# A decoder block on one core: six gate_up blocks with five steps of seven products, six more sets of weight sums made ahead of time, and the rotation's halves exchanged on ScalarE

## The chip, the cores and the metric

The kernel runs on one NeuronCore of a Trainium2 chip, in one launch. The metric is the device time of that launch in microseconds. The engines are named as the profile names them: PE (TensorE, matmuls), PEld (its weight loads), DVE (VectorE), ACT (ScalarE), POOL (GpSimd) and SP (SyncE, which here issues most of the DMA transfers; ACT issues the rest).

## What is computed

One decoder layer for 256 tokens of width 2048, all in float32: a norm, one combined projection to 17,408 columns, three groups of dilated attention with rotary positions, a gated linear recurrence, two branch products under gates, an output product, and a feed-forward network of width 5632. Cut to what the change touches:

```python
def rotary(t, seq_len):
    ...
    rot = jnp.concatenate([-tf[..., half:], tf[..., :half]], axis=-1)
    return (tf * cos + rot * sin).astype(t.dtype)
...
        proj = a @ w_in[layer]
        ...
        y = jax.nn.sigmoid(gate_a) * (attn @ w_attn_branch[layer]) + jax.nn.sigmoid(gate_r) * (r_out @ w_hgrn_branch[layer])
        h = h + rmsnorm(y @ w_mix_out[layer], norm_mix_post[layer])

        a = rmsnorm(h, norm_ffn_pre[layer])
        gt, up = jnp.split(a @ w_ffn_gate_up[layer], [D_FF], axis=-1)
        ...   # silu(gt) * up, times w_ffn_down, norm, added to h
```

## The kernel before

**Products in three parts.** PE multiplies in a reduced form of float32. To keep the precision, each operand is split into a high part (a copy to the reduced type, on ACT) and a low part (the difference, on DVE), and each product is three matmuls: high by high, high by low, low by high. Splitting the weights as they stream in is the steady work of ACT and DVE.

**Wide steps.** The output product and the feed-forward network are computed in wide blocks: two groups of 512 weight columns for all 256 tokens, in steps of 256 rows of the weights. A plain step is 2 token halves x 2 column groups x 2 row tiles, 8 products, 24 matmuls of 128x512. A step "by seven" treats the same as a 2x2 by 2x2 block product in Strassen's manner (Winograd's form): 7 products, 21 matmuls, at the price of sums of weight blocks and of activation blocks. Its weights come in two groups: four sums or blocks split into `w` and `wl`, and three raw blocks split into `dh` and `dl`. `multiply_wide` runs the products with the sums first, then those with the raw blocks, except in a block's last step by seven and in the down product, where the raw ones come first.

**Two ways to get the weight sums.** In the order tables, a step is (row pair, mode): mode 0 is plain; in mode 1 DVE makes the sums when the step is prepared; in mode 2 they were made long before. `weight_sums` does the latter, early in the program: it loads 1 MB of weights, does four DVE operations of 128x512, and stores the set to DRAM through ACT's queue. It is a generator; `ahead_of_time` moves it on by one `yield` for each of the 176 chunks (steps of the first projection and the two branch products). `fetch_sums` brings a set back four steps before it is used.

**The order of the work** is the order in the code; each engine works through its own list. In step i the main loop calls `prepare(i)`, which issues the split of step i + 2, the fetch of sums for step i + 4 and the raw load for step i + 5 (three raw slots), then `multiply(i)`, and then side work. After the second step of each gate_up block, `turn_act` transposes the activations of the block before into two banks of the pool from which the by-seven products get theirs; ACT empties them (L1349), and they are stored. `gather` and `evac_ffn` put the sums of a block together (L510 to L514), then silu and the multiplications (L1385). `dh` and `dl` share room for two steps, `sum` has room for one, `w` and `wl` for three.

**The rotation.** `evac_rope` finishes q and k tiles of 128x512. For the exchanged halves it multiplies 64 partitions of the source by the sine table into the other 64 of the result, twice, on DVE.

In the wide steps of `split_wide` the lines are: L418 (ACT) and L420 (DVE) plain; L426, L427, L429, L430 with fetched sums; L434, L440, L441 (sums on DVE), L439, L442, L445 (ACT), L447, L449 (DVE) with sums on the fly. In the changed kernel these lines stand 15 lower in the file (L420 is L435, L449 is L464), `turn_act`'s L1349 is L1365, L1385 is L1401.

Of the kernel before, what the change touches and what calls it, by code (L numbers as in the profile page):

```python
# [20 lines left out]
P = 128  # L21
S = 256
# [19 lines left out]
    [(2, 0), (3, 0), (0, 1), (4, 0), (1, 1), (5, 0), (6, 0), (7, 0)],  # L42
]
GATE_UP3 = [(3, 0), (4, 0), (0, 2), (5, 0), (1, 1), (6, 0), (2, 2), (7, 0)]
GATE_UP4 = [(4, 0), (5, 0), (0, 2), (6, 0), (1, 1), (2, 2), (3, 1), (7, 0)]
PLACE = (0, 2, 1, 3)
DOWN = [[(m, m in by7) for m in range(KF // 2)] for by7 in (range(4, 20, 3), range(3, 19, 3))]

N_F, N_RAW, N_SPLIT, AHEAD, WARM, BRIDGE = 15, 3, 3, 2, 8, 6

# [50 lines left out]
def tile_hybrid_block(ctx: ExitStack, tc: tile.TileContext, t, out):  # L101
# [13 lines left out]
    def nm(s):  # L115
        serial[0] += 1
        return f"{s}_{serial[0]}"
# [173 lines left out]

    pre, pre_in = {}, {}

    def weight_sums(jobs):

        for n in jobs:
            x = fp[0].tile([P, 2048], F32, tag="pre", bufs=1, name=nm("pre"))
            b, i = steps[n][:2]
            m = b.order[i][0]
            for g in range(2):  # L300
                nc.sync.dma_start(
                    x[:, g * 1024 : (g + 1) * 1024].rearrange("p (k c) -> p k c", k=2),
                    b.w[2 * m * P : (2 * m + 2) * P, b.cols[g] : b.cols[g] + 512]
                    .rearrange("(k p) c -> p k c", p=P),
                )
            for _ in range(4):
                yield
            r = [x[:, q * 512 : (q + 1) * 512] for q in range(4)]
            nc.vector.tensor_sub(r[2], r[2], r[0])
# [6 lines left out]
            nc.scalar.dma_start(pre[n], x)  # L316
            yield

    def fetch_sums(i):
# [7 lines left out]
    def ahead_of_time():  # L327

        if fp and back and not hold[0]:
            advance(back)  # L330

    def split(i):
        if i < len(items):
# [203 lines left out]
    def pair_sums(src, out, slot, pairs=H7):  # L537

        for m in pairs:
            f = ptile("f").rearrange("p (k t) -> p k t", k=2)  # L540
            x = src.slots[m]
            nc.vector.tensor_add(f, x[:, :, 0, :].bitcast(F32), x[:, :, 1, :].bitcast(F32))
            dst = slot().rearrange("p (z n t) -> p z n t", z=2, n=4)
            yield
            for part in seven_sums(f, dst):
                yield
                part()
            out[m] = sums_of(dst)
            yield
# [98 lines left out]
    back, hold = deque(), [False]  # L648
# [46 lines left out]
    def opening():  # L695
        ss, s2 = small("ss"), small("s2")
        yield from sumsq(ss, xt)
        nc.sync.dma_start(gainr, t["hgrn_norm_gain"].to_broadcast([P, HW]))
        nc.sync.dma_start(cs, t["rope"])
        add_parts(s2[:, :2], ss)  # L700
        rsqrt_mean(r1c, s2[:, :2], D)
        ready.add("r1c")
        nc.scalar.preload_act_table_set("silu_and_others")
        yield from row_broadcast(rowb, r1c)
        ready.add("rowb")
        yield
        for _ in range(24):
            yield
        for i, (j, c) in enumerate(((0, -QSCALE), (1, -QSCALE), (0, 1.0), (1, 1.0))):
            nc.vector.scalar_tensor_tensor(  # L710
                out=tabs[:, i, :], in0=cs[:, j, :], scalar=c, in1=rowb, op0=OP.mult, op1=OP.mult
            )
            yield
        nc.sync.dma_start(amask, t["amask"])
        nc.sync.dma_start(lmask, t["lmask"])
# [157 lines left out]
    def evac_rope(key, tab, then=None):  # L873

        cos = tabs[:, tab, :]
        sin = tabs[:, tab + 1, :]

        def ev(i, src):
            if i == 0:
                qkT[key] = fslot("qk").rearrange("p (h t) -> p h t", h=4)  # L880
            yield
            w = ptile("w").rearrange("p (h t) -> p h t", h=2)
            for o, n in ((0, 64), (64, 0)):
                nc.vector.tensor_mul(
                    w[o : o + 64], src[n : n + 64],
                    sin[n : n + 64, None, :].to_broadcast([64, 2, S]),
                )
            yield
            u = src
            nc.vector.tensor_mul(u, src, by_rows(cos, 2))  # L890
            nc.vector.tensor_add(
                qkT[key][:, 2 * i : 2 * i + 2, :].rearrange("p h (two j) -> p h two j", two=2),
                u.rearrange("p h (j two) -> p h two j", two=2),
                w.rearrange("p h (j two) -> p h two j", two=2),
            )
            if i == 1 and then:
                then()
        return ev
# [339 lines left out]
    def mix_to_ffn(i):  # L1238
# [60 lines left out]
        ffn(2, 1)  # L1299
        residual_of(5, (0, 1), False)  # L1300

    def more_h(c):
# [209 lines left out]
    def y_sums():  # L1512
        while not {0, 1} <= yT[0].there:
            yield
        yield from pair_sums(yT[0], y7, lambda: rslot("so"), (0, 1))

    def make_room(c):
        if c == 2:
            flush(evacs)
            flush(back)  # L1520
            end_phase1()

    early = [
# [31 lines left out]
        add("N", w_in, KD, COL_GA + 512 * j, xT, evac_gate(("a", j)))  # L1555
    for j in range(4):
        add("N", t["w_hgrn_branch"][0], 8, 512 * j, lambda k: recT[0](k), evac_rec_branch(j),
            pre=begin_branches if j == 0 else None)
# [13 lines left out]
    add_wide_block(w, (0, FF), PLAIN, lambda k: hT[0](k), None, evac_first, True, mid=more_h)  # L1572
    spare = wides[-1], 0
    for j in range(1, 11):
        add_wide_block(w, (512 * j, FF + 512 * j), GATE_UP4 if j > 1 else GATE_UP3, lambda k: hT[0](k),
                       lambda m: h7[m], evac_ffn, j % 2 == 0,
                       pre=begin_wides if j == 1 else None, turn=1)
    for j in range(2):
# [5 lines left out]
    back.append(  # L1584
        weight_sums([n for n, (b, i, *_) in enumerate(steps) if b.order[i][1] == 2])
    )

    load_x(0, 0, 256)
    load_wide(0, ((0, (0,)), (0, (1,))))
# [8 lines left out]
    split(1)  # L1598
    load_upto(AHEAD + N_RAW - 1)
    for i in range(len(items)):  # L1600
        kind, n, _ = items[i]
# [99 lines left out]
```

## Time and profile before

| | |
|---|---|
| median of 3 runs | 1697.41 us (1697.04 to 1697.93) |
| the profiled execution | 1698.13 us |
| its span | 1696.3 us |
| PE / PEld / DVE / ACT busy | 99% / 84% / 85% / 54% |
| granted TensorE clock, mean | 0.998 |
| DMA | 413.48 MB, 244 GB/s over the span |

Times in the profile are microseconds from the start of the span; the launch takes 1.8 us besides. The chunks end near 1000 us, then come the output product, eleven gate_up blocks (the first all plain) up to about 1455, two down blocks, and the end with its norm and stores from 1682. A row of a timeline gives start, duration, engine, line, operation, output and inputs, and in brackets the idle time ahead of it and what ended it.

### The profile page before, as it was taken

What the parts mean: (1) busy time and instruction counts of PE and PEld (TensorE: products, weight loads), DVE (VectorE), ACT (ScalarE), POOL (GpSimd) and SP (SyncE); (2) the same over time, 40 slices, a digit from 0 to 9 for tenths busy, and PEclk for the clock granted to TensorE, in tenths of its full rate; (3) what the DMA queues carried; (4) which work ended last, traced back from release to release, by engine and by line L of the source; (5) the groups of instructions that cost most, each with busy time, mean ns of one, the idle gap of its engine ahead of it and who ended that gap; (6) DMA issues with size and microseconds to landing.
All of it is one profiled execution on the core that took longest, in us unless ns stands there. A gap on an engine that the chain in (4) does not pass through costs nothing.

```text
span 1696.3 us, 21711 instructions
## 1 busy us (share of the span) xinstructions
PE 1685.2 (99%) x8260; PEld 1416.7 (84%) x8260; DVE 1436.2 (85%) x1662; ACT 914.7 (54%) x1034; POOL 3.9 (0%) x13
## 2 busy tenths in 40 slices
PE   9999999999999999999999999999999999999997
PEld 7888888888888888888888888888888888888886
DVE  6999888867998988885668888888888888898997
ACT  6655555544444434445445547555555555565663
POOL 0000000000000000000000000000000000000000
PEclk9999999999999999999999999999999999999999
DMA  8667666768677767787858646777777777777773
GB/s 285 205 224 243 230 233 228 234 222 309 225 254 252 256 223 243 253 310 275 295 172 275 210 162 227 269 250 252 254 255 253 249 248 272 257 266 256 248 244 130
DMA packets 228904, 413.48 MB, mean 244 GB/s; under 512 B 12816, under 2 KB 79552, under 8 KB 226240
## 3 DMA queue, kind: packets, MB, share of 16 engines
q1 hardware_dynamic: 218544, 373.93, 65.4%
q10 hardware_dynamic: 10192, 38.15, 6.0%
q8 instruction: 64, 1.05, 0.3%
q14 instruction: 40, 0.33, 0.1%
q0 software_dynamic: 64, 0.02, 0.0%
HBM read 376.92 MB, written 35.13 MB: 243 GB/s over the span
## 4 chain that ended last, share of the span: by engine, by line
PE 98%; DVE 1%; ACT 0%; issue 0%; DVEq 0%; ACTq 0%
PE acc L138 62%; PE aux L138 34%; PE aux L930 0%; DVE wl L420 0%; PE aux L610 0%; PE aux L1348 0%; DVE fz L1475 0%; PE acc L1348 0%; ACT w L418 0%; ACT junk L1429 0%; PE aux L597 0%; DVE e L1425 0%; PE aux L1110 0%; DVE yT L578 0%; PE aux L1220 0%
## 5 line engine op out<-in xcount | busy, mean ns | idle before, releaser
L138 PE MATMUL acc<-xT,w 128*128 128x256 f32 (+1 forms) x2048 | 366.8, 338 | 0.0
L420 DVE TENSOR_TENSOR wl<-raw,w 128x2048 fp32r<-128x2048 f32 (+1 forms) x141 | 306.6, 2182 | 68.8 <-ACT w L418 67.1
L138 PEld LDWEIGHTS acc<-xT,w 128*128 128x128 f32 x2048 | 311.9, 188 | 44.7 <-DVE w L365 0.3
L418 ACT ACTIVATE w<-raw 128x2048 fp32r<-128x2048 f32 (+1 forms) x141 | 256.3, 1827 | 109.3 <-PE acc L138 35.1
L364 ACT ACTIVATE w<-raw 128x1024 fp32r<-128x1024 f32 x176 | 185.7, 1058 | 220.5 <-PE acc L138 169.6
L365 DVE TENSOR_TENSOR w<-raw,w 128x1024 fp32r<-128x1024 f32 x176 | 214.8, 1221 | 95.9 <-ACT w L364 95.2
L138 PE MATMUL acc<-w,xT 128*128 128x512 f32 x578 | 169.1, 392 | 0.0
L439 ACT ACTIVATE w<-sum 128x1024 fp32r<-128x1024 f32 x56 | 59.5, 1063 | 177.8 <-DVE sum L434 170.6
L138 PE MATMUL acc<-w,hT 128*128 128x512 f32 x472 | 152.7, 391 | 0.4 <-DVE hT L1232 0.4
L447 DVE TENSOR_TENSOR wl<-sum,w 128x1024 fp32r<-128x1024 f32 x112 | 134.8, 1221 | 13.2 <-ACT w L439 13.2
L138 PEld LDWEIGHTS acc<-w,xT 128*128 128x128 f32 x578 | 108.1, 188 | 22.2
L138 PE MATMUL aux<-w,hT 128*128 128x512 f32 x374 | 120.0, 389 | 0.0
L449 DVE TENSOR_TENSOR dl<-raw,dh 128x1536 fp32r<-128x1536 f32 x56 | 98.3, 1756 | 14.3 <-ACT dh L445 12.2
L138 PE MATMUL aux<-w,xT 128*128 128x512 f32 x344 | 109.8, 389 | 0.0
L138 PEld LDWEIGHTS acc<-w,hT 128*128 128x128 f32 x472 | 88.5, 188 | 19.0 <-DVE hT L1232 0.8
L138 PE MATMUL acc<-wl,hT 128*128 128x512 f32 x236 | 91.9, 389 | 0.0
L445 ACT ACTIVATE dh<-raw 128x1536 fp32r<-128x1536 f32 x56 | 82.7, 1476 | 8.0 <-PE aux L138 4.4
L138 PE MATMUL acc<-w,a 128*128 128x512 f32 x268 | 83.7, 389 | 0.0
L138 PE MATMUL aux<-w,a 128*128 128x512 f32 x268 | 83.7, 389 | 0.0
L138 PEld LDWEIGHTS aux<-w,hT 128*128 128x128 f32 x374 | 70.2, 188 | 14.6
L138 PE MATMUL acc<-w,so 128*128 128x512 f32 x234 | 78.8, 391 | 0.0
L138 PEld LDWEIGHTS aux<-w,xT 128*128 128x128 f32 x344 | 64.6, 188 | 13.4
(298 smaller groups left out, 2964.3 us busy)
## 6 DMA issues: line engine op xcount, KB each, us to landing
raw<-in_w_in SPq DMA_DIRECT2D x270, 512.0 KB, 4.8
raw<-in_w_ffn_gate_up SPq DMA_DIRECT2D x156, 512.0 KB, 4.8
raw<-in_w_ffn_down SPq DMA_DIRECT2D x88, 512.0 KB, 5.4
pre<-in_w_ffn_gate_up SPq DMA_DIRECT2D x40, 512.0 KB, 6.5
presum<-pre ACTq DMA_DIRECT2D x20, 1024.0 KB, 4.7
s<-presum SPq DMA_DIRECT2D x40, 512.0 KB, 7.0
raw<-in_w_mix_out SPq DMA_DIRECT2D x32, 512.0 KB, 4.9
act<-acts SPq DMA_DIRECT2D x22, 512.0 KB, 6.5
```

The source lines that it names most:

```text
L138: nc.tensor.matmul(ps, lhsT, rhs, start=start, stop=stop, skip_group_check=True)
L364: nc.scalar.activation(wh, raw, AF.Copy)
L365: nc.vector.tensor_sub(wl, raw, wh.bitcast(F32))
L418: nc.scalar.activation(hi[:, c], raw[:, c], AF.Copy)
L420: nc.vector.tensor_sub(lo[:, c], raw[:, c], hi[:, c].bitcast(F32))
L439: nc.scalar.activation(hi[:, :1024], s[:, :1024], AF.Copy)
L445: nc.scalar.activation(dhi, d, AF.Copy)
L447: nc.vector.tensor_sub(lo[:, c], s[:, c], hi[:, c].bitcast(F32))
L449: nc.vector.tensor_sub(dlo, d, dhi.bitcast(F32))
```

## The change

1. A new table GATE_UP5 with five steps by seven in a row, used for gate_up blocks 3, 4, 6, 7, 9 and 10 (blocks 2, 5 and 8 keep GATE_UP4 with four). Three of its five use sums made ahead of time, where GATE_UP4 has two, so 26 sets are made in place of 20.
2. The second down block has seven steps by seven in place of six, and takes over the activation sums that the first block made for the same rows.
3. In the rotation ACT copies the two halves across, and DVE multiplies all 128 partitions once; the signs move into the tables.
4. `weight_sums` starts a set every six chunks in place of seven once the first q is there, on odd chunks. The last two sets are made by a second worker, `beside`, in half tiles, from the second recurrence branch block on.
5. One more pair of activation sums of the normed rows.

```diff
+GATE_UP5 = [(5, 0), (6, 0), (0, 2), (1, 1), (2, 2), (4, 2), (3, 1), (7, 0)]
 GATE_UP4 = [(4, 0), (5, 0), (0, 2), (6, 0), (1, 1), (2, 2), (3, 1), (7, 0)]
-DOWN = [[...] for by7 in (range(4, 20, 3), range(3, 19, 3))]
+DOWN = [[...] for by7 in (range(4, 20, 3), (2, 4, 7, 10, 13, 16, 18))]
...
-    def weight_sums(jobs):
+    def weight_sums(jobs, halves=False):
         for n in jobs:
-            x = fp[0].tile([P, 2048], F32, tag="pre", bufs=1, name=nm("pre"))
+            quick = not halves and ("q", 0, 0) in qkT
+            while quick and count[0] % 2 == 0:
+                yield
+            if halves:
+                xs = [fslot("pre") for _ in range(2)]
+            else:
+                x = fp[0].tile([P, 2048], F32, tag="pre", bufs=1, name=nm("pre"))
+                xs = [x[:, g * 1024 : (g + 1) * 1024] for g in range(2)]
...
-            for _ in range(4):
+            for _ in range(3 if halves or quick else 4):
                 yield
...
         if fp and back and not hold[0]:
             advance(back)
+        if fp and beside[0]:
+            advance(beside[0])
...
-        for i, (j, c) in enumerate(((0, -QSCALE), (1, -QSCALE), (0, 1.0), (1, 1.0))):
+        for i, (j, c) in enumerate(((0, -QSCALE), (1, QSCALE), (0, 1.0), (1, -1.0))):
...
             for o, n in ((0, 64), (64, 0)):
-                nc.vector.tensor_mul(
-                    w[o : o + 64], src[n : n + 64],
-                    sin[n : n + 64, None, :].to_broadcast([64, 2, S]),
-                )
+                nc.scalar.activation(w[o : o + 64], src[n : n + 64], AF.Copy)
             yield
             u = src
             nc.vector.tensor_mul(u, src, by_rows(cos, 2))
+            nc.vector.tensor_mul(w, w, by_rows(sin, 2))
...
-            lanes[1].append(pair_sums(hT[0], h7, lambda: rslot("so"), range(4)))
+            lanes[1].append(pair_sums(hT[0], h7, h7_slot, range(5)))
...
-        if by7:
+        if by7 and m not in a7:
...
+    def begin_beside(c):
+        if c == 0:
+            beside[0] = deque([weight_sums(jobs[-2:], True)])
...
-        add_wide_block(..., GATE_UP4 if j > 1 else GATE_UP3, ...)
+        order = GATE_UP3 if j == 1 else GATE_UP5 if j in (3, 4, 6, 7, 9, 10) else GATE_UP4
+        add_wide_block(..., order, ...)
```

What each engine is given, in order, at three places. The first is ACT's list in gate_up block 3, from the silu of the block before (L1382, in the changed kernel L1398) on; `act` is the tile into which the two transposed banks go. Before:

```order
L1382 ACTIVATE e_9257<-e_9257,r2c 128x512
L1382 ACTIVATE e_9258<-e_9258,r2c 128x512
L426 ACTIVATE w_9301<-s_9227 128x1024
L426 ACTIVATE w_9301<-s_9228 128x1024
L429 ACTIVATE dh_9307<-raw_9199 128x1536
L418 ACTIVATE w_9344<-raw_9231 128x2048
L1349 ACTIVATE act_9379<-acc_9380 128x512
L1349 ACTIVATE act_9379<-acc_9386 128x512
```

And after the change, the same stretch:

```order
L1398 ACTIVATE e_9349<-e_9349,r2c 128x512
L1398 ACTIVATE e_9350<-e_9350,r2c 128x512
L441 ACTIVATE w_9393<-s_9319 128x1024
L441 ACTIVATE w_9393<-s_9320 128x1024
L444 ACTIVATE dh_9399<-raw_9291 128x1536
L454 ACTIVATE w_9440<-sum_9442 128x1024
L457 ACTIVATE w_9440<-sum_9442 128x1024
L460 ACTIVATE dh_9448<-raw_9323 128x1536
L1365 ACTIVATE act_9485<-acc_9486 128x512
L1365 ACTIVATE act_9485<-acc_9492 128x512
```

One copy that needs only a raw tile stood ahead of the two emptying copies; now three stand there, and two of them need sums from DVE.

The second is DVE's list in the same block, from the sums of the first on-the-fly step to the low part of the last one. Before:

```order
L434 TENSOR_TENSOR sum_9396<-raw_9268 128x1024
L440 TENSOR_TENSOR sum_9396<-raw_9268,sum_9396 128x512
L441 TENSOR_TENSOR sum_9396<-raw_9268,sum_9396 128x512
L447 TENSOR_TENSOR wl_9395<-sum_9396,w_9394 128x1024 x2
L449 TENSOR_TENSOR dl_9403<-raw_9268,dh_9402 128x1536
L427 TENSOR_TENSOR wl_9437<-s_9348,w_9436 128x1024
L427 TENSOR_TENSOR wl_9437<-s_9349,w_9436 128x1024
L430 TENSOR_TENSOR dl_9443<-raw_9311,dh_9442 128x1536
L434 TENSOR_TENSOR sum_9475<-raw_9352 128x1024
```

After, from the first on-the-fly step's low parts on:

```order
L462 TENSOR_TENSOR wl_9441<-sum_9442,w_9440 128x1024 x2
L464 TENSOR_TENSOR dl_9449<-raw_9323,dh_9448 128x1536
L442 TENSOR_TENSOR wl_9501<-s_9403,w_9500 128x1024
L442 TENSOR_TENSOR wl_9501<-s_9404,w_9500 128x1024
L445 TENSOR_TENSOR dl_9507<-raw_9360,dh_9506 128x1536
L442 TENSOR_TENSOR wl_9539<-s_9454,w_9538 128x1024
L442 TENSOR_TENSOR wl_9539<-s_9455,w_9538 128x1024
L445 TENSOR_TENSOR dl_9545<-raw_9407,dh_9544 128x1536
L449 TENSOR_TENSOR sum_9574<-raw_9458 128x1024
```

Between the two on-the-fly steps there are now two with fetched sums, and the `dl` of the second stands directly ahead of the last step's sums.

The third is SP's list near the end of the chunks, where `pre` are the loads of `weight_sums`, `raw` those of the chunks, and `gate` fetches of stored gates. Before:

```order
L269 DMA raw_6863<-in_w_hgrn_branch 128x2x512 x2
L301 DMA pre_6911<-in_w_ffn_gate_up 128x2x512 x2
L858 DMA gate_6914<-waits_1557 128x2x512
L269 DMA raw_6919<-in_w_hgrn_branch 128x2x512 x2
L858 DMA gate_6958<-waits_1560 128x2x512
L269 DMA raw_6963<-in_w_hgrn_branch 128x2x512 x2
L269 DMA raw_7012<-in_w_attn_branch 128x2x512 x2
L269 DMA raw_7072<-in_w_attn_branch 128x2x512 x2
```

After:

```order
L270 DMA raw_6961<-in_w_hgrn_branch 128x2x512 x2
L309 DMA pre_6986<-in_w_ffn_gate_up 128x2x512
L309 DMA pre_6987<-in_w_ffn_gate_up 128x2x512
L873 DMA gate_7008<-waits_1560 128x2x512
L270 DMA raw_7013<-in_w_hgrn_branch 128x2x512 x2
L309 DMA pre_7059<-in_w_ffn_gate_up 128x2x512 x2
L270 DMA raw_7067<-in_w_attn_branch 128x2x512 x2
L270 DMA raw_7128<-in_w_attn_branch 128x2x512 x2
L309 DMA pre_7174<-in_w_ffn_gate_up 128x2x512
L309 DMA pre_7175<-in_w_ffn_gate_up 128x2x512
L270 DMA raw_7181<-in_w_attn_branch 128x2x512 x2
L309 DMA pre_7228<-in_w_ffn_gate_up 128x2x512 x2
```

Four loads of sums (two of them in halves, the second worker's) now stand between the last raw loads of the recurrence branch and those of the attention branch, where one stood.

More of the change, by code (lines that the diff above doesn't have):

```diff
@@ L44 @@
 GATE_UP3 = [(3, 0), (4, 0), (0, 2), (5, 0), (1, 1), (6, 0), (2, 2), (7, 0)]
+GATE_UP5 = [(5, 0), (6, 0), (0, 2), (1, 1), (2, 2), (4, 2), (3, 1), (7, 0)]
 GATE_UP4 = [(4, 0), (5, 0), (0, 2), (6, 0), (1, 1), (2, 2), (3, 1), (7, 0)]
 PLACE = (0, 2, 1, 3)
-DOWN = [[(m, m in by7) for m in range(KF // 2)] for by7 in (range(4, 20, 3), range(3, 19, 3))]
+DOWN = [[(m, m in by7) for m in range(KF // 2)] for by7 in (range(4, 20, 3), (2, 4, 7, 10, 13, 16, 18))]
 N_F, N_RAW, N_SPLIT, AHEAD, WARM, BRIDGE = 15, 3, 3, 2, 8, 6
@@ L301, in weight_sums @@
                 nc.sync.dma_start(
-                    x[:, g * 1024 : (g + 1) * 1024].rearrange("p (k c) -> p k c", k=2),
+                    xs[g].rearrange("p (k c) -> p k c", k=2),
                     b.w[2 * m * P : (2 * m + 2) * P, b.cols[g] : b.cols[g] + 512]
@@ L305, in weight_sums @@
                 )
-            for _ in range(4):
+            for _ in range(3 if halves or quick else 4):
                 yield
-            r = [x[:, q * 512 : (q + 1) * 512] for q in range(4)]
+            r = [xs[q // 2][:, q % 2 * 512 : (q % 2 + 1) * 512] for q in range(4)]
             nc.vector.tensor_sub(r[2], r[2], r[0])
@@ L315, in weight_sums @@
             pre[n] = dram.tile([P, 2048], F32, name=nm("presum"))
-            nc.scalar.dma_start(pre[n], x)
+            if halves:
+                for g in range(2):
+                    nc.scalar.dma_start(pre[n][:, g * 1024 : (g + 1) * 1024], xs[g])
+                yield
+            else:
+                nc.scalar.dma_start(pre[n], x)
             yield
@@ L647, in tile_hybrid_block @@
     evacs, turns, lanes, queue = deque(), deque(), [deque(), deque()], deque()
-    back, hold = deque(), [False]
+    back, hold, beside, count = deque(), [False], [None], [0]
     ready = set()
@@ L1300, in mix_to_ffn, with h7_slot @@
         residual_of(5, (0, 1), False)
+    def h7_slot():
+        return p3("so", F32R, 1024, 4) if len(h7) < 4 else rslot("so")
     def more_h(c):
@@ L1520, in make_room @@
             flush(back)
+            flush(beside[0])
             end_phase1()
@@ L1557, in tile_hybrid_block @@
         add("N", t["w_hgrn_branch"][0], 8, 512 * j, lambda k: recT[0](k), evac_rec_branch(j),
-            pre=begin_branches if j == 0 else None)
+            pre=begin_branches if j == 0 else None, post=begin_beside if j == 1 else None)
     for j in range(4):
@@ L1574, in tile_hybrid_block @@
     for j in range(1, 11):
-        add_wide_block(w, (512 * j, FF + 512 * j), GATE_UP4 if j > 1 else GATE_UP3, lambda k: hT[0](k),
+        order = GATE_UP3 if j == 1 else GATE_UP5 if j in (3, 4, 6, 7, 9, 10) else GATE_UP4
+        add_wide_block(w, (512 * j, FF + 512 * j), order, lambda k: hT[0](k),
                        lambda m: h7[m], evac_ffn, j % 2 == 0,
@@ L1583, in tile_hybrid_block @@
     wides[-3].post = lambda c: fetch_act(c // 2) if c in (1, 3) else None
-    back.append(
-        weight_sums([n for n, (b, i, *_) in enumerate(steps) if b.order[i][1] == 2])
-    )
+    jobs = [n for n, (b, i, *_) in enumerate(steps) if b.order[i][1] == 2]
+    back.append(weight_sums(jobs[:-2]))
     load_x(0, 0, 256)
@@ L1600, in tile_hybrid_block @@
     for i in range(len(items)):
-        kind, n, _ = items[i]
+        count[0], (kind, n, _) = i, items[i]
         b, c = kind[n][:2]
```

## The prediction

> **What bounds the kernel now.** I read the page's totals first, then PE's list of waits, then the chain.
>
> ```profile
> span 1696.3 us, 21711 instructions
> PE 1685.2 (99%) x8260; PEld 1416.7 (84%) x8260; DVE 1436.2 (85%) x1662; ACT 914.7 (54%) x1034; POOL 3.9 (0%) x13
> PE 98%; DVE 1%; ACT 0%; issue 0%; DVEq 0%; ACTq 0%
> PE aux L138 <- DVE warm L162: 1.2, 1, 1.2
> PE acc L138 <- DVE hT L1232: 0.4, 1, 0.4
> PE acc L138 <- DVE gate L1147: 0.2, 1, 0.2
> 1163.09 10.88 PE acc L138 x48
> ```
>
> PE works 1685.2 of 1696.3 us and all its named waits come to 1.8 us, so PE's own work is the time: a matmul less is a gain, and every new wait of PE is a loss at its full length. The last row is two plain steps in the chain: 48 matmuls of 128x512 in 10.88 us, 0.2267 us each. A plain step (24) costs 5.44 us, a step by seven (21) costs 4.76, so a replaced step gives 0.68. Seven are replaced, six in gate_up and one in the down product: 7 x 0.68 = 4.76 us. These are the only matmuls that the change takes away. What is left to find is which waits come in for them.
>
> **A gate_up block with five steps by seven.** I take FFN block 4 of the trace, from 1162.9 us, as the pattern, and move its rows as the new order asks.
>
> ```profile
> 1189.00:1231.00 42.00, 42.00 (x191) 34.88 (x190) 36.78 (x33) 24.14 (x21) 0.00 (x0) 1.00 0.73 253
> 1169.47 1.28 DVE L1385 TENSOR_TENSOR e<-e,e 128x512 f32<-128x512 f32 x2
> 1170.67 2.28 DVE L420 TENSOR_TENSOR wl<-raw,w 128x2048 fp32r<-128x2048 f32 x1
> 1184.98 1.22 DVE L434 TENSOR_TENSOR sum<-raw 128x1024 f32<-128x1024 f32 x1
> 1186.23 0.69 DVE L440 TENSOR_TENSOR sum<-raw,sum 128x512 f32<-128x512 f32 x1
> 1186.95 0.69 DVE L441 TENSOR_TENSOR sum<-raw,sum 128x512 f32<-128x512 f32 x1
> 1181.04 2.35 DVE L427 TENSOR_TENSOR wl<-s,w 128x1024 fp32r<-128x1024 f32 x2
> 1183.31 1.75 DVE L430 TENSOR_TENSOR dl<-raw,dh 128x1536 fp32r<-128x1536 f32 x1
> 1187.56 2.44 DVE L447 TENSOR_TENSOR wl<-sum,w 128x1024 fp32r<-128x1024 f32 x2
> 1191.15 1.76 DVE L449 TENSOR_TENSOR dl<-raw,dh 128x1536 fp32r<-128x1536 f32 x1 [1.16 <-ACT dh L445]
> ```
>
> The first row is one block period (us, then busy PE, PEld, DVE, ACT, POOL, the granted clock, DMA share, GB/s). DVE works 36.78 of 42.0 us. The new block trades a plain split (L420, 2.28) for a split with fetched sums (L427 and L430, 2.35 + 1.75 = 4.10): 38.6 of 41.3 us, 93%. On average it fits; the order decides whether each result is in time.
>
> *Place A, the third step.* The block's fourth step is now one that makes its sums on the fly; before it was plain. ACT does that split ahead of the two copies that empty the banks of the transposes, and PE wants the first of those banks for the seventh matmul of step 3.
>
> ```profile
> 1174.44 1.09 ACT L1349 ACTIVATE act<-aux 128x512 f32<-128x512 f32 x2 [3.91 <-PE aux L1348]
> 1175.83 0.62 PE L138 MATMUL aux<-w,so 128*128 128x512 f32 x2
> 1186.29 1.06 ACT L439 ACTIVATE w<-sum 128x1024 fp32r<-128x1024 f32 x1 [3.69 <-DVE sum L434]
> 1187.68 1.06 ACT L442 ACTIVATE w<-sum 128x1024 fp32r<-128x1024 f32 x1 [0.33 <-DVE sum L441]
> 1177.85 1.48 ACT L445 ACTIVATE dh<-raw 128x1536 fp32r<-128x1536 f32 x1
> ```
>
> Now the copies start at 1174.44, and ACT had been idle 3.91 us. In the new order DVE can begin the sums where the plain subtraction stood, 1170.67, behind the multiplications of L1385. The rows of the later step give the offsets: sums end 2.66 us after their start (1186.95 + 0.69 - 1184.98), at 1173.33; the second copy of sums starts 0.04 later, 1173.37, dh about 0.96 on, 1174.33; the first emptying copy follows some 1.4 later, 1175.7, and takes a half of 1.09 to 0.6, 1176.3. PE wants the bank at 1175.83 + 0.23 = 1176.06. A wait of 0.25 to 0.3 us. Bounds: 0, if DVE starts its sums 0.3 earlier than here, and 0.57, if the raw tile is late by as much again (place C). I take 0.30: 6 x 0.30 = 1.80 us.
>
> *Place B, the last step by seven.* The parts dh and dl have room for two steps. Before, the steps by seven stood three in a row at most; now there are five. Let S be the end of the fourth step of the block (the second by seven).
>
> ```profile
> 1189.63 1.49 ACT L445 ACTIVATE dh<-raw 128x1536 fp32r<-128x1536 f32 x1 [0.89 <-PE aux L138]
> 1189.66 0.39 PE L138 MATMUL aux<-w,so 128*128 128x512 f32 x1
> 1194.64 0.39 PE L138 MATMUL acc<-dl,hT 128*128 128x512 f32 x1
> ```
>
> The first row is such a wait for room: ACT starts dh as PE's step ends (next step's first matmul at 1189.66). dl followed it at 1191.15 and was done at 1192.91, and PE wanted it at 1194.64: 1.73 us to spare. In the new order the sixth step's dh waits for S; its dl follows at S + 1.5 on DVE. Only then, in DVE's order, come the seventh step's sums (start S + 3.2, end S + 5.85), its second copy on ACT (S + 5.9), dh (S + 6.8 to 8.3), and dl (S + 8.35 to 10.1). The seventh step begins with the products of the raw weights, so PE wants dl at its second matmul, S + 2 x 4.76 + 0.23 = S + 9.75. A wait of 0.35 to 0.4 us; bounds 0 and 0.6 by the same rows with the gaps seen between them left out or doubled. I take 0.38: 6 x 0.38 = 2.28 us.
>
> *Place C, the block behind.* The raw tile of the next block's second step may be loaded only when that late dl has been read.
>
> ```profile
> 1192.94 0.88 SPq L287 DMA_DIRECT2D raw<-in_w_ffn_gate_up  x2
> raw<-in_w_ffn_gate_up SPq DMA_DIRECT2D x2, 512.0 KB, 4.1
> raw<-in_w_ffn_gate_up SPq DMA_DIRECT2D x156, 512.0 KB, 4.8
> 1199.38 1.92 ACT L418 ACTIVATE w<-raw 128x2048 fp32r<-128x2048 f32 x1 [2.12 <-PE acc L138]
> ```
>
> The load was issued 0.03 us after dl's end, its second half about 0.4 later, and landed 4.1 (these two) to 4.8 us (all) after that: S + 14.6 to 15.3. ACT's split is otherwise let in by PE, 4.7 us behind dl's wanted time in these rows (1199.38 against 1194.64), about S + 14.9 with the wait at B. So 0 to 0.5 us late, which reaches PE only where place A is tight too: in blocks 4, 7 and 10, which follow a block of five. I take 0.2: 3 x 0.2 = 0.60. The other four blocks have plain steps in those places, and time to make up what is late. The six more sets to fetch are 6 MB on SP's queue over ten blocks at share 0.73 of the DMA engines; I cost them at nothing, covered by the two steps of lead with which sums are fetched. More activation sums (one more pair for the normed rows) fall in the all-plain opening block, where DVE's fixed work is 8 x 2.2 of 43.5 us: nothing.
>
> **The down product.** One step more by seven.
>
> ```profile
> 1571.00:1696.00 125.00, 116.03 (x512) 95.73 (x511) 111.51 (x141) 68.54 (x78) 0.00 (x0) 0.98 0.60 205
> ```
>
> This row is the second block with the tail, where DVE has 13.5 us free. The step adds 1.22 + 2 x 0.69 + 2.44 + 1.76 - 2.28 = 4.5 us to DVE, and the activation sums of five steps are no longer made again. Its gain stays: -0.68, already in the 4.76. Bounds of a wait here: 0 to 0.3; I take 0.
>
> **The work ahead of time.** Six more sets, in less time for each, and the rotation's halves on ACT.
>
> ```profile
> 525.00:575.00 50.00, 50.00 (x289) 43.54 (x288) 46.62 (x70) 23.07 (x33) 0.00 (x0) 1.00 0.71 243
> L365 DVE TENSOR_TENSOR w<-raw,w 128x1024 fp32r<-128x1024 f32 x96 | 117.0, 1220 | 32.0 <-ACT w L364 31.4
> L884 DVE TENSOR_TENSOR w<-sum,tabs 64x512 f32<-64x512 f32 x46 | 31.6, 687 | 1.0
> 613.67 1.02 SPq L301 DMA_DIRECT2D pre<-in_w_ffn_gate_up  x2
> 621.94 0.69 DVE L309 TENSOR_TENSOR pre<-pre 128x512 f32<-128x512 f32 x1 [0.40 <-issue]
> pre<-in_w_ffn_gate_up SPq DMA_DIRECT2D x40, 512.0 KB, 6.5
> ```
>
> The 525 to 575 row shows the tight part: DVE 93% busy, ACT 46%. A rotation costs DVE two multiplications of half the partitions (0.687 each) now and one of all of them after, 0.69 saved, 24 times: 16.6 us. Six sets at four times 0.69 cost 16.6 us. So DVE comes out even, and ACT, with half its time free, takes 48 small copies. A chunk lasts 315/96 = 3.28 us (the rows of L365 and L884 are from 437 to 752 us). A set's first subtraction now comes 8.3 us after its loads' issue and once waited 0.40 us; one chunk earlier it comes after 5.0, with 6.5 us and half the 1.02 of issue to wait for, so DVE stands some 2.0 us. About 2.5 sets fall into 50 us: 5 us, against 3.4 free and 2.5 saved by 3.65 rotations. It about fits, but the wait stands in front of chunk splits that PE wants soon. Bounds -0.5 (DVE freed of the rotations) to +6; near the lower one, +0.5.
>
> ```profile
> 792.00:812.00 20.00, 20.00 (x102) 16.93 (x101) 11.65 (x13) 10.48 (x14) 0.00 (x0) 1.00 0.93 304
> 812.00:832.00 20.00, 20.00 (x100) 16.89 (x99) 13.07 (x21) 10.46 (x14) 0.00 (x0) 1.00 1.01 363
> 832.00:852.00 20.00, 20.00 (x104) 17.04 (x104) 12.57 (x19) 8.53 (x12) 0.00 (x0) 1.00 0.62 203
> 852.00:872.00 20.00, 20.00 (x98) 16.84 (x97) 10.98 (x13) 8.11 (x9) 0.00 (x0) 1.00 0.53 178
> ```
>
> The last sets fall from 832 to 872 us, where SP's queue has the raw loads behind theirs. Three sets read and written are 6.3 MB on top of 7.6: 13.9 MB in 40 us, 348 GB/s. The row at 812 moved 363 with PE never idle, so I take +0.2; bounds 0 and, if only the 304 of the row at 792 can be had, 13.9 MB / 304 - 40 = +5.7.
>
> **The sum** against the profiled execution (1698.13 us, span 1696.3): -4.76 + 1.80 + 2.28 + 0.60 + 0.5 + 0.2 = +0.62, so 1698.75. The median of the runs, 1697.41, lies 0.72 below that execution; as a median I predict 1698.0.
>
> **Rivals.** (1) Only PE counts: the new waits at A and B are not there, as each rests on offsets of a few tenths. For it: PE is 99% busy. Against it: DVE at 93% in such a block, and a chain of single results. The gain is then whole, 1697.41 - 4.76 = 1692.65; with 0.7 lost in the early work, 1693.3. The Trainium skill ("Perfetto Trace Analysis", section "Identifying the Most-Contended Engine") says to improve first the engine with the highest occupancy, and by that rule this rival's time would come out; it also counts TensorE by its weight loads, here 84% beside DVE's 85%, by which DVE would be no less the bound. No row here decides between the two.
> (2) Slower, by the transfers of 832 to 872 us: the loads of sums stand ahead of raw loads on SP's queue, and it decides from where a raw load slips by more than its lead. A chunk there is 12 matmuls, 2.72 us, and three raw slots less 4.8 us of landing leave 3.4 us. The price is 5.7 less 3.4 to 5.7 whole, middle 4.0: 1698.0 + 4.0 = 1702.0. For it: share 0.93 at only 304 GB/s; against it: 363 right after. The Trainium skill (same page, section "Engine Utilization") puts the 16 DMA engines at some 435 GB/s for one active core; by that figure 348 would leave room and this rival would fall, but share 1.01 at 363 here speaks against taking it.
> (3) Slower, by the closer sets in the rotations' stage: beyond 2.4 us of wait for a set (5.9 free / 2.5) DVE falls behind. At 3.7 us (0.40 + 3.3) it loses 2.5 x 3.7 - 5.9 = 3.3 in 50 us, over the hundred tight microseconds 6.6; half of the sets so, about +3.5: 1701.5.
>
> **Chances.** Forecast 0.55, with its own range 1696.0 to 1700.5 (A and B together from 2.0 to 5.8). Rival 1 0.20, rival 2 0.13, rival 3 0.08, others 0.04, halved to both sides. What a measurement here tells from no change is about 0.2%, 3.4 us: faster 0.22, same 0.55, slower 0.23. The range for 8 in 10 takes in rival 1 after the early loss and most of rivals 2 and 3: 1693.0 to 1702.3.
>
> **What would show it.** Right: PE waits of 0.25 to 0.6 us once in each of blocks 3, 4, 6, 7, 9, 10 for ACT's emptying copy (now L1365), and of 0.3 to 0.5 for dl (L464); the period of such a block 42.0 us or a little less. Wrong: periods near 41.3 and no such waits (rival 1); PE waits or gaps from 832 to 875 us for a split whose raw load is late (rival 2), or from 525 to 640 us for L365's successor behind a waiting subtraction of a set (rival 3). A wait in the down product, or a changed clock, would be something that I have not priced.

## The result and the profile after

The changed kernel takes 1713.26 us (median of 4 runs, 1711.83 to 1714.02), the kernel before 1697.67 (4 runs): 1.009 of it, interval 1.0078 to 1.0103. The prediction was 1698.0 with a range to 1702.3, so the change costs 15.6 us where +0.6 was forecast. The profiled execution took 1712.61 us.

The page of the changed kernel, the totals and the chain:

```profile
span 1710.8 us, 21793 instructions
PE 1687.3 (99%) x8239; PEld 1410.2 (82%) x8239; DVE 1444.3 (84%) x1665; ACT 953.8 (56%) x1093; POOL 3.9 (0%) x13
PE 78%; DVE 8%; issue 5%; DMA 5%; ACT 3%; SPq 0%; DVEq 0%; ACTq 0%
```

PE runs 21 matmuls less, as foretold, and the span is 14.5 us longer. PE's share of the chain fell from 98% to 78%: DVE and DMA have come into it. PE's waits, first from 400 to 1000 us, then from 1000 on (in total, times, longest):

```profile
PE acc L139 <- DVE w L380: 6.1, 9, 1.4
PE aux L139 <- DVE q L1053: 1.1, 1, 1.1
...
PE acc L139 <- DVE e L1395: 1.2, 1, 1.2
PE aux L139 <- ACT act L1365: 1.0, 2, 0.5
PE acc L139 <- DVE dl L464: 0.8, 3, 0.3
PE aux L139 <- DVE dl L464: 0.8, 3, 0.3
PE acc L139 <- ACT act L1365: 0.5, 1, 0.5
```

The second group holds the waits for the emptying copy (L1365, place A) and for dl (L464, place B), six for dl and three for the copy above the list's threshold. The first group is the larger loss: nine waits for L380, DVE's low part of a chunk's weights, while the sets are made. The first matmul of the output product, which follows the chunks, puts a date on it: it starts at 903.10 us before and at 913.82 after (the chunks end there, near 900 us and not near 1000). The changed kernel is 10.7 us behind at that point, having been 0.8 ahead at 340 us, so the early work lost 11.5 us; the other 3.8 come behind it. Why L380 is late, in four rows of DVE, ACT and SP around 580 us, one of DVE at 842 us, the chain of waits from 831 us (start, length, what), SP's wait ahead of the set's load at 538 us (in total, times, longest), and the loads issued at 830 us (KB each, us to landing):

```profile
573.20 2.62 SPq L309 DMA_DIRECT2D pre<-in_w_ffn_gate_up  x2
585.39 0.69 DVE L317 TENSOR_TENSOR pre<-pre 128x512 f32<-128x512 f32 x1 [4.12 <-DMA pre<-in_w_ffn_gate_up]
586.72 1.22 DVE L380 TENSOR_TENSOR w<-raw,w 128x1024 fp32r<-128x1024 f32 x1
589.75 2.22 ACT L379 ACTIVATE w<-raw 128x1024 fp32r<-128x1024 f32 x2 [6.11 <-DVE pre L321]
...
842.20 0.69 DVE L317 TENSOR_TENSOR pre<-pre,pre 128x512 f32<-128x512 f32 x1 [8.30 <-DMA pre<-in_w_ffn_gate_up]
...
831.07 9.56 DMA presum<-pre
840.69 5.45 DMA pre<-in_w_ffn_gate_up
...
SPq L309 <- DMA presum<-pre: 2.5, 1, 2.5
...
pre<-in_w_ffn_gate_up SPq DMA_DIRECT2D x2, 512.0 KB, 11.1
```

DVE reaches a set's first subtraction (L317) before the set has landed and stands 4.12 and 8.30 us. Behind it in DVE's list are the low parts of chunks (L380), and ACT stands too, since its list has the set's store, which needs DVE's last operation (6.11 us ahead of L379). The chain shows one cause of a late load: it may not be issued until the set before has been stored, and that store took 9.56 us. The load of 538.26 us was held so for 2.5 us, and DVE stood 2.41 us for it. The last row shows another cause: these loads had been issued and took 11.1 us. The windows of two stretches, 525 to 600 us and that of the last sets, 832 to 892, each for the kernel before and then for the changed one (columns as in the prediction):

```profile
525.00:600.00 75.00, 75.00 (x444) 65.65 (x443) 71.35 (x105) 32.42 (x44) 0.00 (x0) 1.00 0.76 255
...
525.00:600.00 75.00, 71.34 (x414) 61.05 (x414) 65.64 (x97) 37.55 (x55) 0.00 (x0) 1.00 0.72 243
...
832.00:892.00 60.00, 60.00 (x296) 50.45 (x296) 39.53 (x53) 25.45 (x32) 0.00 (x0) 1.00 0.55 181
...
832.00:892.00 60.00, 56.62 (x270) 45.54 (x269) 41.36 (x57) 23.35 (x30) 0.00 (x0) 1.00 0.93 322
```

From 525 to 600 us PE loses 3.7 us of busy time at no higher a DMA share. From 832 on the share rises from 0.55 to 0.93, and PE loses 3.4 us in the 60.

### The profile page after: what moved, and what is told of

Read it like the earlier page. It is cut to its first block, busy times and chain, and to the rows that moved or that the text cites. A ratio compares the mean times of both kernels' runs of the same rounds, so it can differ in the third digit from the quotient of the medians.

```text
span 1710.8 us, 21793 instructions
## 1 busy us (share of the span) xinstructions
PE 1687.3 (99%) x8239; PEld 1410.2 (82%) x8239; DVE 1444.3 (84%) x1665; ACT 953.8 (56%) x1093; POOL 3.9 (0%) x13
## 4 chain that ended last, share of the span: by engine, by line
PE 78%; DVE 8%; issue 5%; DMA 5%; ACT 3%; SPq 0%; DVEq 0%; ACTq 0%
PE acc L139 49%; PE aux L139 28%; DMA presum<-pre 3%; DMA pre<-in_w_ffn_gate_up 2%; DVE w L380 1%; ACT w L433 1%; DVE sum L449 1%; DVE wl L435 1%; DVE e L1395 1%; ACT dh L444 1%; ACT dh L460 1%; DVE sum L455 0%; DVE sum L456 0%; DMA raw<-in_w_in 0%; DVE e L1401 0%
## 5 line engine op out<-in xcount | busy, mean ns | idle before, releaser
L139 PE MATMUL acc<-xT,w 128*128 128x256 f32 (+1 forms) x2048 | 368.2, 338 | 2.9 <-DVE w L380 2.9
L139 PEld LDWEIGHTS acc<-xT,w 128*128 128x128 f32 x2048 | 311.7, 188 | 49.2 <-DVE w L380 5.0
L435 DVE TENSOR_TENSOR wl<-raw,w 128x2048 fp32r<-128x2048 f32 (+1 forms) x134 | 290.8, 2178 | 64.1 <-ACT w L433 62.3
L433 ACT ACTIVATE w<-raw 128x2048 fp32r<-128x2048 f32 (+1 forms) x134 | 242.9, 1822 | 98.3 <-PE acc L139 29.3
L379 ACT ACTIVATE w<-raw 128x1024 fp32r<-128x1024 f32 x176 | 185.0, 1057 | 190.0 <-PE acc L139 102.9
L380 DVE TENSOR_TENSOR w<-raw,w 128x1024 fp32r<-128x1024 f32 x176 | 214.3, 1221 | 80.5 <-ACT w L379 80.2
L139 PE MATMUL acc<-w,xT 128*128 128x512 f32 x578 | 169.5, 392 | 0.1
L139 PE MATMUL acc<-w,hT 128*128 128x512 f32 x430 | 139.8, 391 | 0.4 <-DVE hT L1245 0.4
L139 PEld LDWEIGHTS acc<-w,xT 128*128 128x128 f32 x578 | 108.0, 188 | 22.7 <-DVE w L380 0.6
L139 PE MATMUL aux<-w,xT 128*128 128x512 f32 x344 | 109.8, 389 | 0.0
L464 DVE TENSOR_TENSOR dl<-raw,dh 128x1536 fp32r<-128x1536 f32 x57 | 100.2, 1757 | 9.2 <-ACT dh L460 7.1
L139 PE MATMUL aux<-w,hT 128*128 128x512 f32 x332 | 107.1, 389 | 0.0
L139 PEld LDWEIGHTS acc<-w,hT 128*128 128x128 f32 x430 | 80.7, 188 | 17.4 <-DVE hT L1245 0.8
L139 PE MATMUL acc<-w,so 128*128 128x512 f32 x258 | 87.7, 392 | 0.8 <-ACT act L1365 0.5
L139 PE MATMUL acc<-w,a 128*128 128x512 f32 x268 | 83.8, 389 | 1.2 <-DVE e L1395 1.2
L139 PE MATMUL acc<-wl,hT 128*128 128x512 f32 x215 | 83.7, 389 | 0.0
L139 PE MATMUL aux<-w,so 128*128 128x512 f32 x240 | 81.7, 392 | 1.1 <-ACT act L1365 1.0
L139 PE MATMUL aux<-w,a 128*128 128x512 f32 x254 | 79.4, 389 | 0.0
L139 PEld LDWEIGHTS aux<-w,xT 128*128 128x128 f32 x344 | 64.6, 188 | 13.4
```

The costliest lines, as they stand in the source:

```text
L139: nc.tensor.matmul(ps, lhsT, rhs, start=start, stop=stop, skip_group_check=True)
L379: nc.scalar.activation(wh, raw, AF.Copy)
L380: nc.vector.tensor_sub(wl, raw, wh.bitcast(F32))
L433: nc.scalar.activation(hi[:, c], raw[:, c], AF.Copy)
L435: nc.vector.tensor_sub(lo[:, c], raw[:, c], hi[:, c].bitcast(F32))
L464: nc.vector.tensor_sub(dlo, d, dhi.bitcast(F32))
```

## The experiments

Each is set against the kernel before, timed beside it, whose median was 1697.5 to 1697.8 in all of them. They are told in an order that follows the argument.

**The two halves of the loss.** The first kernel keeps the later blocks and puts the early work back (20 sets at the old pace; steps without a set of their own take another's):

```diff
+    reuse = {n: jobs[k] for k, n in enumerate(jobs[20:])}
+    jobs = jobs[:20]
...
-            quick = not halves and ("q", 0, 0) in qkT
+            quick = False
```

> The changed kernel with the early work as before: 20 sets of weight sums at the old pace, no second worker; the rotation stays on ScalarE and all later blocks stay changed (six steps fetch another step's set, so six sets are left out). Theory M (the closer sets and the second worker lose the early 11.5 us; the later blocks lose 3.8): the early loss is gone, 1697.7 + 3.8 = 1701.5, within 1700.5 to 1703. Rival R (the rotation's copies on ScalarE lose the 5 us between 540 and 600 us): 1706 or more.

Measured: 1701.77 us (ratio 1.0023, 1.0014 to 1.0032). The second keeps the early work and puts the later blocks back (`order = GATE_UP3 if j == 1 else GATE_UP4`, the old down table):

> The changed kernel with gate_up and down blocks as before (GATE_UP4, six steps by seven in the second down block), all 26 sets still made, six of them unused. Theory M: the early loss stays whole, 1697.7 + 10.7 = 1708.4, within 1707 to 1710, and no wait of PE in the gate_up blocks. If the loss came from the later blocks: near 1698.

Measured: 1709.15 us (1.0068, 1.0056 to 1.0081). +4.1 and +11.4 make 15.5 of the 15.6: the parts add up. The third is the kernel before with the rotation alone:

> The kernel before with the rotation's halves on ScalarE alone. Theory M: no loss, 1697.7 within 0.7 (DVE has 0.69 us less per rotation, PE waited for nothing there). Rival R: the copies stand ahead of splits on ScalarE's list, so 2 to 5 us more, 1700 to 1703.

Measured: 1697.94 us (1.0001, 0.9992 to 1.0009). The rotation costs nothing and gives nothing; the early loss is that of the sets.

**What in the sets.** Without the second worker (`beside[0] = deque()`, 24 sets):

> The changed kernel without the second worker: 24 sets at the new pace, two steps fetch another step's set (two sets are left out). Theory M: of the early 11.5 us the 5 between 540 and 600 us stay, the 5.4 between 840 and 875 us shrink to 1 or less, since the two workers no longer stand in one another's way on the queues: 1713.3 - 4.7 = 1708.6. Rival: the new pace alone fills the queues there, and no more than 1 us is won: 1712.3.

Measured: 1707.29 us (1.0057, 1.0043 to 1.0071). Its windows and PE's waits in the early work (its lines stand one lower in the file, L381 is L380):

```profile
832.00:892.00 60.00, 60.00 (x296) 50.51 (x296) 42.68 (x58) 25.31 (x32) 0.00 (x0) 1.00 0.77 263
...
PE acc L139 <- DVE w L381: 1.4, 3, 1.0
PE aux L139 <- DVE q L1054: 1.1, 1, 1.1
```

PE loses nothing any more from 832 to 892 us; what stays, 3.5 us by the trace, lies between 540 and 600 us. So the two last sets, with the worker that makes them, cost the late loss. (Up to 800 us this kernel does what the changed one does, whose profile lost 6.1 us there: the early loss differs by some 2.5 us from one execution to another.) Next, the sets' four DVE operations a chunk later and in one piece, at the same pace:

```diff
-            for _ in range(3 if halves or quick else 4):
+            for _ in range(4):
                 yield
...
-            yield
+            if not (halves or quick):
+                yield
```

> The changed kernel with each set's four DVE operations a chunk later and in one piece; the pace (six chunks for a set), the number of sets and all transfers stay. Theory L (DVE stands in front of chunk splits because a set's loads wait for the store of the set before and land after the first subtraction's place): the 5 us between 540 and 600 us shrink to 1.5 or less, and of the 5.4 at 840 to 875 us half go: 1713.3 - 6 = 1707.3. Rival P (the pace itself, DVE's or the transfers' load, is too high there): 1712.5 to 1714.

Measured: 1707.92 us (1.0060, 1.0048 to 1.0073). The same work at the same pace loses 5.3 us less when DVE comes to it later: the standing in front of a late load costs that much, and DVE's load is the same. Some 6 of the 11.5 us stay by its trace, so this run does not show that the standing is all of it. Then the stores issued by GpSimd (`nc.gpsimd.dma_start(pre[n], x)`):

> The changed kernel with the stores of the sets issued by GpSimd in place of ScalarE. Theory L with both engines standing (ScalarE's list waits at the store for DVE's late operations, with chunk splits behind it): 2 to 4 of the early 11.5 us go, 1710.5. If only DVE's standing counts (the low parts come from DVE anyway): no more than 1 us, 1712.5 to 1714.

Measured: 1710.27 us (1.0071, 1.0057 to 1.0085). ACT's standing behind the store is worth about 3 us of it (its runs spread from 1708.02 to 1712.94), between 540 and 600 us; the late loss stays. Then only one set stored:

> The changed kernel with one store: the first set alone is stored and every later step with fetched sums takes it (25 stores are left out; loads and DVE operations stay). Theory L (a set's loads wait for the store before, land late, and DVE stands): the loads start some 5 to 8 us sooner against DVE's place, and the early 11.5 us shrink to 2 or less: 1703.5. Rival P (DVE's own load is too high): the loss stays, 1712 or more. Between them, 1707 to 1710, if what is late is as much the loads' own landing, beside the fetches of values, as the wait for the store.

Measured: 1702.54 us (1.0028, 1.0017 to 1.0040): with 10.7 us less, the early loss is gone (0.55 us left by the trace). That takes two things away at once, the wait of a load for the store before it and the stores' own traffic. So a kernel with as many bytes stored, read from another tile, for which no load has to wait:

```diff
-                nc.scalar.dma_start(pre[n], x)
+                for g in range(2):
+                    nc.scalar.dma_start(pre[n][:, g * 1024 : (g + 1) * 1024], tabs.rearrange("p a t -> p (a t)"))
```

> The changed kernel with every set's store reading the rotation's tables in place of the set (two stores of 512 KB each, so the same 26 MB are moved; what later steps fetch is not the sums). The loads of the next set then wait for no store, and ScalarE's list for no DVE operation of a set. Theory L (the wait of loads for the store, and the two lists that stand): the early loss nearly goes as with one store, 1702.5 to 1704. Rival T (the stores' traffic makes the loads and the chunks' raw loads late): the loss stays in great part, 1708 to 1712.

Measured: 1709.49 us (1.0061, 1.0048 to 1.0075). Theory L alone is not enough: by the medians 3.8 us go with the waits, and some 7 stay with the traffic. Windows from 832 us and the loads issued at 836 us, of this kernel (KB each, us to landing), and the same windows with one store:

```profile
832.00:892.00 60.00, 57.46 (x278) 46.97 (x277) 43.15 (x61) 22.91 (x28) 0.00 (x0) 1.00 0.89 317
pre<-in_w_ffn_gate_up SPq DMA_DIRECT2D x2, 512.0 KB, 12.2
```

```profile
832.00:892.00 60.00, 60.00 (x297) 50.45 (x296) 49.88 (x69) 25.36 (x32) 0.00 (x0) 1.00 0.68 235
```

At a share of 0.89 a load takes 12.2 us from its issue; at 0.68 PE loses nothing. The single runs of this kernel spread from 1705.65 to 1710.47, those of the kernel before over 0.9 us, and its profile has 3.4 us at a granted clock of 0.50 (last section), an estimated 1.7 us of what stays. No run of the three kernels overlaps with another's, so the waits and the traffic both count; the split into 3.8 and 7 is good to 2 us or so, and which of them is the larger stays open.

**The gate_up blocks.** The order of the five steps alone is changed:

```diff
-GATE_UP5 = [(5, 0), (6, 0), (0, 2), (1, 1), (2, 2), (4, 2), (3, 1), (7, 0)]
+GATE_UP5 = [(5, 0), (6, 0), (0, 2), (2, 2), (1, 1), (3, 1), (4, 2), (7, 0)]
```

> The changed kernel with the five steps by seven in another order: (0,2), (2,2), (1,1), (3,1), (4,2). The fourth step's split then needs no sums from DVE ahead of the emptying copies (place A), and the last step needs none behind a late dl (place B). Theory M (A and B are matters of order): the 6.96 us that the traces show there go, and some of the 1.3 at the start of the down product, 1713.3 - 7 to 8 = 1705.5 to 1706.5. Rival D (DVE's load in such a block is the bound, whatever the order): 1711 to 1713.

Measured: 1707.96 us (1.0064, 1.0050 to 1.0077), 5.3 less and not 7 to 8. PE's waits after 1000 us, the end of its last gate_up block, and the windows around it:

```profile
PE acc L139 <- DVE e L1395: 2.2, 1, 2.2
PE acc L139 <- DVE dl L445: 0.7, 1, 0.7
PE acc L139 <- DVE hT L1245: 0.4, 1, 0.4
...
1461.87 0.47 PE L139 MATMUL acc<-w,a 128*128 128x512 f32 x1 [2.19 <-DVE e L1395]
1463.23 0.63 PE L139 MATMUL acc<-wl,a 128*128 128x512 f32 x1
1463.66 1.05 PE L139 MATMUL acc<-w,a 128*128 128x512 f32 x2
...
1462.00:1465.50 3.50, 3.50 (x10) 2.74 (x11) 1.51 (x3) 3.00 (x4) 0.00 (x0) 0.56 0.89 282
```

Places A and B are gone from all blocks but the last, where DVE also has the down product's activations to split. It comes 2.19 us late to the sums that free the banks, and after that idle time PE works at a granted clock of 0.56 for 3.5 us. With the five-step blocks moved so that the last gate_up block has four (and the early work as in the first experiment):

```diff
-GATE_UP5 if j in (3, 4, 6, 7, 9, 10)
+GATE_UP5 if j in (2, 3, 5, 6, 8, 9)
```

> The order of the last run, the blocks with five steps moved to 2, 3, 5, 6, 8 and 9 so that the last gate_up block has four, and the early work with 20 sets at the old pace (six steps fetch another step's set, six sets are left out). Theory M: all waits of the gate_up blocks go, and so does the one at the start of the down product: 6 x 0.68 = 4.08 and 0.49 for the second down block, 1697.7 - 4.6 = 1693.1, within 1692.4 to 1694. Rival D (DVE falls behind wherever two such blocks follow each other): a wait of about 1 us in blocks 3, 6 and 9, so 1696.

Measured: 1693.33 us (0.9975, 0.9965 to 0.9984), theory M to 0.2 us. With order and place right, six blocks with five steps give nearly their full gain: from block 1 to block 10 the trace has 371.7 us for 375.2 before, 3.6 of the 4.1, and one wait for dl of 0.2 us. How far this goes was tried with three on-the-fly steps of the five, which need no further set, `(0, 2), (2, 2), (1, 1), (3, 1), (4, 1)` in blocks 3, 5, 7 and 9:

> A version without any further set: the early work with 20 sets at the old pace; gate_up blocks 3, 5, 7 and 9 take five steps by seven of which three make their sums on the fly: (0,2), (2,2), (1,1), (3,1), (4,1); seven steps by seven in the second down block. DVE then has 36.8 + 6.8 - 2.3 = 41.3 us of work for 41.0 in such a block, and 36.8 of 41.7 in the block behind it. Theory M (order decides, the next block makes it up): 4 x 0.68 + 0.49 = 3.2 less than before, 1694.4. Rival D (a block over its period makes PE wait): a wait of 0.5 to 1 us in each, 1697 to 1698.5.

Measured: 1705.26 us (1.0044, 1.0032 to 1.0057). Rival D, and dearer than it said:

```profile
PE aux L140 <- DVE dl L465: 5.2, 4, 1.3
PE aux L140 <- ACT dh L461: 3.1, 4, 0.8
```

Two waits in each of the four blocks (the lines stand two or one lower here): 8.3 us, before PE's time to start again. Load and order are not told apart here. The three on-the-fly steps stand in a row, and DVE takes 6.85 us for each (two begin their sums at 1226.01 and 1232.86) where PE takes 4.76 for a step; in the first of them it stood 1.32 us for a dh that had no room yet. So 38.6 us of DVE's work in a block of 41.0 do fit in a good order; that 41.3 fit in none is not shown.

**Two versions meant to be faster.** The first has 22 sets at the old pace:

> A version meant to be faster, complete: 22 sets at the old pace and no second worker, the new order in gate_up blocks 4 and 7 alone, seven steps by seven in the second down block, the rotation on ScalarE. Theory M: no early loss (two more sets fall where the transfers have room, 850 to 890 us), 2 x 0.68 + 0.49 = 1.85: 1695.9. If two more sets already fill the queues there: 1697 to 1699.

Measured: 1705.63 us (1.0047, 1.0034 to 1.0059). A miss of its own making: one wait, `PE acc L139 <- ACT w L379: 6.8, 1, 6.8`, at 870 us. The last set was not done when the pools change, where the rest of a worker runs in one go, so its operations stood right behind its loads. The second makes 23 sets, at the new pace outside the stretch from about 500 to 600 us, the last done in time:

```diff
-            quick = not halves and ("q", 0, 0) in qkT
+            quick = ("q", 0, 0) in qkT and not 118 < count[0] < 145
...
-GATE_UP5 if j in (3, 4, 6, 7, 9, 10)
+GATE_UP5 if j in (3, 6, 8)
```

> A version meant to be faster, complete: 23 sets, no second worker, the new pace outside the stretch of about 500 to 600 us and the old one in it, the last set done before the change of pools; the new order in gate_up blocks 3, 6 and 8, seven steps by seven in the second down block, the rotation on ScalarE. 3 x 0.68 + 0.49 = 2.53 less than before: 1695.1. If the pace in the rest of the early work loses too (0.6 us near 750 us in the changed kernel): 1696.

Measured: 1695.10 us (11 runs, 0.9984, 0.9975 to 0.9993): faster than both kernels, by 2.7 us (0.16%; its slowest run, 1695.89, is below the fastest of the kernel before, 1697.15) and by 18 us. Its windows there and its only waits:

```profile
832.00:892.00 60.00, 60.00 (x296) 50.41 (x296) 43.52 (x59) 25.35 (x33) 0.00 (x0) 1.00 0.69 234
PE aux L625 <- DMA x<-in_x: 1.4, 1, 1.4
PE aux L139 <- DVE warm L163: 1.2, 1, 1.2
PE acc L139 <- DVE hT L1245: 0.4, 1, 0.4
PE acc L139 <- DVE gate L1160: 0.2, 1, 0.2
```

## Where the prediction was right and where it was wrong

**The work ahead of time (+0.7 forecast, +11.4 measured): the step that failed.** Two terms of the sum were mis-sized: +0.5 for the sets in the rotations' stretch and +0.2 for those from 832 to 872 us. Both took a mean over a stretch (DVE's free time, the transfers' rate) for what one late load does to the list behind it.
- For the stretch of the rotations I let a load land 6.5 us after its issue, and its issue stand where the list has it. The pair issued from 573.20 on took until 585.3, 12 us, beside fetches of values, and other loads of sets waited at SP for a store (8 waits between 525 and 900 us, 23.3 us in all, for 3 and 6.0 before). DVE then stood 2.41 and 4.12 us, not 2.0, and ACT stood with it, which I had not listed at all: the set's store is in ACT's list ahead of chunk splits. I set DVE's standing against its free time, and on that mean it did fit: from 525 to 600 us its work and the two stands are 65.64 + 2.41 + 4.12 = 72.2 of 75 us. PE lost its 3.7 us all the same, since the splits right behind each stand came late, and for their lead the sum had no term. The term was about 5 us. That is rival 3, priced at 3.5 and given 0.08.
- For 832 to 872 us I took a rate seen once without harm (363 GB/s) as proof that 348 would do. From 832 to 852 us 349 GB/s were reached; single transfers became late. A pair of loads issued at 830.12 landed in some 11 us, in place of the 6.5 of the page before, and DVE stands in front of such a load whatever the mean rate is. That is rival 2 in its place and its price, 4.0 for 5.4 measured, but not in its mechanism: it had raw loads slip by more than their lead. Raw loads did land late, up to 11.9 us after their issue between 828 and 880 us, but no wait of DVE, ACT or PE there names one; DVE stood for loads of sets, 13.2 us in two waits. Rival 2 was given 0.13 for the sake of one row of an average. The Trainium skill ("Perfetto Trace Analysis", section "Engine Utilization") has 435 GB/s for one active core; by that figure there was room, and this trace shows PE losing 3.4 us at 322 GB/s and a share of 0.93.
- Rivals 2 and 3 were treated as excluding one another. They came together, and in both places the trace has the same step, DVE in front of a set's load that has not landed. That closer sets are behind both is argued: without the second worker the late loss went and the early one stayed.

**The gate_up blocks (+0.6 with the gain forecast, +2.9 measured).** Places A and B are where they were said to be, and nearly as late. At B, PE's matmuls before and after the wait start 0.64 us apart in place of 0.23, that is 0.41 late for 0.38 forecast. What I left out is that PE needs about 0.11 more to start again:

```profile
1163.21 0.39 PE L139 MATMUL aux<-dh,hT 128*128 128x512 f32 x1
1163.85 0.50 PE L139 MATMUL aux<-dl,hT 128*128 128x512 f32 x1 [0.25 <-DVE dl L464]
1164.19 0.39 PE L139 MATMUL aux<-dh,hT 128*128 128x512 f32 x1
```

The second matmul's successor starts 0.34 behind it. So a wait that the profile names 0.25 costs 0.52. Over a pair of such blocks, by the instruction that begins to gather a block's sums (first and last start, before and after, blocks 2 and 4):

```profile
L510 ACT ACTIVATE e<-aux x2: 600/600/600, 1113.3 to 1196.7; 128x512 f32<-128x512 f32 x2
L525 ACT ACTIVATE e<-aux x2: 598/599/600, 1124.0 to 1208.3; 128x512 f32<-128x512 f32 x2
```

83.4 us became 84.3 where 1.36 had been gained: 2.3 us of waits a pair, 6.9 in all, for 4.68 in the sum. Place C showed as a longer wait at A in the second block of a pair (0.49 of idle time for 0.13). I also called the window of 42.0 us a block's period, which is 41.7 by these rows; nothing in the sum hung on it.

**The down product (-0.68 forecast, +0.9 measured).** The cost of places A and B was priced in PE's waits alone. DVE leaves the last block late as well, the sums that free the banks for the down product come late (L1395), and PE waits 1.16 there. That follow-on was in no term. The second down block gave 0.49 of its 0.68.

**The matmuls (-4.76) and the rotation** were right: with the waits nearly out of the way, six blocks and the down step gave 4.25 of 4.76 (1697.58 to 1693.33).

## What to carry to other kernels

When PE is busy 99% of the time, what a change saves is known at once and what it costs is in the lists of the other engines: go through each result that is now needed sooner or made later, and add PE's restart to each wait. Work put into spare time costs nothing only while its data are there when the engine comes to it; in a list worked in order, price the standing in front of a late transfer with everything behind it, on every queue that the transfer and its store pass. A mean rate that was once reached says little on how late a single transfer will be: leave room, or place the consumer later.

## What was not expected of the hardware

After 2.19 us of idle time PE ran at a granted clock of 0.56 for 3.5 us: matmuls of 128x512 started 0.43 us apart (1463.23 to 1463.66) in place of 0.23. After 1.16 us, in the changed kernel at 1469.69, it did not. The length of the gap does not decide this alone. Behind 1.82 us in the run with GpSimd's stores, and behind 1.12 us in the run that stored the tables, the clock fell too (the two rows below); behind 1.11 us at 594.73 in the changed kernel it stayed at 1.00.

```profile
872.00:875.50 3.50, 3.50 (x11) 2.69 (x10) 3.46 (x5) 0.00 (x0) 0.53 (x1) 0.51 0.93 271
594.80:598.20 3.40, 3.40 (x13) 2.92 (x12) 3.40 (x7) 1.26 (x2) 0.00 (x0) 0.50 0.91 298
```

The Trainium skill ("TensorE: Matmul & The Clock Gate", Part 1) gives 426.7 ns for such a matmul at the low clock, which agrees, and an idle window of some 3.4 us before it drops; here shorter gaps were enough. So the wait of 2.19 us cost some 1.6 us more than itself (eight matmuls at 0.2 us each).
